# A first group of six products instead of four, fed by one load for each k-tile

## The chip, the cores and the metric

The kernel runs on one core of a Trainium2 chip. A core has TensorE (PE: matrix products and the loads of their weights), ScalarE (ACT), VectorE (DVE), GpSimd (POOL) and SyncE (SP, which issues most loads). The metric is the device time of one execution in microseconds (us), the median of several executions. The granted clock of TensorE averaged 0.995 of full speed, which is the 2.4 GHz level, in the profiled execution.

## What is computed

One inference step of a hybrid decoder layer for 256 prompt tokens and 8 sample tokens that share the weights. With NT = 264 columns of tokens and D = 2048:

```python
def _rmsnorm(x, g):
    x32 = x.astype(jnp.float32)
    y = x32 * lax.rsqrt(jnp.mean(x32 * x32, axis=-1, keepdims=True) + EPS) * g.astype(jnp.float32)
    return y.astype(x.dtype)
# h   = RMSNorm(x)
# z   = h @ w_in      (columns for the mLSTM heads, the sliding-window attention heads, two merge gates)
# A   = mLSTM matrix memory (4 heads, dk=256, dv=512)
# B   = sliding-window attention (32 query heads, 4 key/value heads, head_dim 64, window 128),
#       with sinks and partial rotary
# mix = (sigmoid(gA) * (A @ w_branch_a) + sigmoid(gB) * (B @ w_branch_b)) @ w_out
# x   = x + RMSNorm(mix)
# x   = x + RMSNorm(ConvFFN(RMSNorm(x)))
```

All is in 32-bit floating point. The kernel reaches that precision with three products for each weight tile: weights and activations are split into a rounded high part (`wh`, `xh`) and a remainder (`wl`, `xl`), and `wh·xh + wh·xl + wl·xh` is summed.

## The kernel before

Weights lie in memory as tiles of 128 x 128: an output tile of 128 columns has 16 of them, one for each k-tile of D. The function `product` (L86 to L117) makes n output tiles. It goes through chunks of at most eight weight tiles. For each chunk SP issues one load into `raw` (one of three buffers; L100), ACT casts `raw` to `wh` (L102), DVE forms `wl` as raw minus wh (L103), and PE does three matmuls of 128 x 128 by 128 x 264 for each tile into the accumulator `acc` (L111, L112, L113). `one` is `product` with a single output tile: two chunks of eight.

After a full chunk of eight `product` calls `step()`. It moves on the work that is dealt out between products: generators in `running`, each of which does a piece and yields, and generators in `waiting`, which are started one by one, seven steps apart (`launch` with a gap of 7). `drain` runs all that is left to its end, with no products between the pieces. The instructions of each engine are put into their final order by a scheduler that goes by priorities and by a model of durations.

The first group (L179) makes two key and two value tiles at once, in chunks of one k-tile, one, and then two. `load_x` issues the load of the pieces of x that the chunk needs, just ahead of the chunk's weights, on the same queue, and makes `xh` (ACT, L173) and `xl` (DVE, L174), with the weights of the norm in `gv`. The squares of x are summed into `xacc` (ACT L159, L162; DVE L163). Then `rstd_from` forms the reciprocal root mean square: 12 small matmuls `rs` (L147), a root on ACT, four steps on DVE (`rq`), matmuls and transposes that spread it over the columns (`rb`, L216, L218), and a copy to `rstd`. The tables of rotary cosines and sines in `katt` are multiplied by rstd (L232, L233). Keys go through `rope` (DVE and POOL), values through transposes `vt` (L266) into `VHL`.

Next come 16 products for the queries, four to a group g. Each goes through `rope` into `Qh` and `Ql`. After each group two generators `half` are launched, which do the attention of the prompt: scores `s` (L288, L290), softmax on ACT, transposes, products with the values, and at the end `hah` and `hal`, the split of the attention's output. Behind the eight of them `sample_attention` is launched, for the 8 sample tokens: scores `ss` (L369), softmax `es` and `Ps` (L379, L381), transposes `pst`, products `psp` and `psv` (L399, L404), sums and copies `hs` on DVE (L410, L412, L417) and the splits into `hah` and `hal`. Then follow the mLSTM gates, 16 products of the gate gB (their result is kept in `Bp`), and the products `qk_products(0)` for the first mLSTM head. Then `drain()` is called, four sigmoids of `Bp` are done on ACT (L748), and 16 products with the weights `wb` take `hah` and `hal` in place of `xh` and `xl`. ACT has the functions of its tables loaded in sets: a change from the exponential to the sigmoid shows as an `ACT_TABLE_LOAD`.

## Time and profile before

| | us |
|---|---|
| median of 3 executions | 1783.11 (1782.82 to 1787.02) |
| profiled execution, device time | 1782.28 |
| its span, first to last instruction | 1780.5 |
| PE busy in the span | 1749.1 |
| DVE busy | 1222.0 |
| ACT busy | 830.4 |
| first product matmul starts at | 5.07 |
| first matmul with hah starts at | 299.63 |

The span begins with the first instruction; what lies outside of it is 1.8 us. Busy time of an engine counts what it executes; a matmul's row lasts about 0.28 us, but matmuls overlap, so what a matmul costs is the distance from start to start. In the rows, a bracket at the end is the idle time of the engine before the instruction and what ended it; "<-" between two names reads "made from".

### The profile page before, as it was taken

What the parts mean: (1) busy time and instruction counts of PE and PEld (TensorE: products, weight loads), DVE (VectorE), ACT (ScalarE), POOL (GpSimd) and SP (SyncE); (2) the same over time, 40 slices, a digit from 0 to 9 for tenths busy, and PEclk for the clock granted to TensorE, in tenths of its full rate; (3) what the DMA queues carried; (4) which work ended last, traced back from release to release, by engine and by line L of the source; (5) the groups of instructions that cost most, each with busy time, mean ns of one, the idle gap of its engine ahead of it and who ended that gap; (6) DMA issues with size and microseconds to landing.
All of it is one profiled execution on the core that took longest, in us unless ns stands there. A gap on an engine that the chain in (4) does not pass through costs nothing.

```text
span 1780.5 us, 35035 instructions
## 1 busy us (share of the span) xinstructions
PE 1749.1 (98%) x14188; PEld 1733.7 (97%) x14188; DVE 1222.0 (69%) x2271; ACT 830.4 (47%) x1160; POOL 248.2 (14%) x438
## 2 busy tenths in 40 slices
PE   8999999999999999999999999999999999999996
PEld 8999999999999999999999899999999999999996
DVE  7788866556888798756643887777777777444443
ACT  6556555334555455444445544444444444434442
POOL 2542010000111121100021320000000001000001
PEclk9999999999999999999999999999999999999998
DMA  7444475655888888955555445555555555566563
GB/s 250 161 143 142 155 232 169 224 182 189 273 280 284 317 299 298 311 194 184 179 180 176 148 159 179 180 182 183 187 179 185 181 179 184 184 180 185 179 184 114
DMA packets 106587, 354.82 MB, mean 199 GB/s; under 512 B 11626, under 2 KB 20730, under 8 KB 106424
## 3 DMA queue, kind: packets, MB, share of 16 engines
q1 hardware_dynamic: 91672, 300.05, 51.0%
q0 software_dynamic: 14752, 52.52, 8.6%
q8 instruction: 111, 1.82, 0.4%
q14 instruction: 52, 0.43, 0.1%
HBM read 328.21 MB, written 24.32 MB: 198 GB/s over the span
## 4 chain that ended last, share of the span: by engine, by line
PE 84%; DVE 5%; DMA 5%; issue 2%; ACT 2%; POOL 2%; SPq 0%; POOLq 0%; ACTq 0%; DVEq 0%
PE acc L111 27%; PE acc L112 26%; PE acc L113 26%; DMA raw<-in_w_in 4%; DVE wl L103 2%; ACT wh L102 1%; POOL xs L847 1%; DMA katt<-in_katt 1%; DVE Ct L730 1%; PE s L288 0%; PE nc L668 0%; POOL qr L240 0%; PE pt L326 0%; DVE cj L733 0%; DMA out_c_s<-Ct 0%
## 5 line engine op out<-in xcount | busy, mean ns | idle before, releaser
L103 DVE TENSOR_TENSOR wl<-raw,wh 128x1024 fp32r<-128x1024 f32 (+1 forms) x569 | 694.5, 1221 | 418.3 <-ACT wh L102 414.9
L102 ACT CAST wh<-raw 128x1024 fp32r<-128x1024 f32 (+1 forms) x569 | 588.8, 1035 | 805.4 <-PE acc L112 587.4
L111 PE MATMUL acc<-xh,wh 128*128 128x264 f32 x1600 | 456.0, 285 | 2.8 <-ACT wh L102 2.8
L113 PE MATMUL acc<-xh,wl 128*128 128x264 f32 x1600 | 453.0, 284 | 1.9 <-DVE wl L103 1.8
L112 PE MATMUL acc<-xl,wh 128*128 128x264 f32 x1600 | 454.1, 284 | 0.1
L111 PE MATMUL acc<-h2h,wh 128*128 128x264 f32 x1408 | 399.9, 284 | 5.6 <-DVE E L862 3.4
L112 PE MATMUL acc<-h2l,wh 128*128 128x264 f32 x1408 | 401.2, 285 | 2.1 <-DVE h2l L852 1.9
L113 PE MATMUL acc<-h2h,wl 128*128 128x264 f32 x1408 | 399.7, 284 | 0.0
L111 PEld LDWEIGHTS acc<-xh,wh 128*128 128x128 f32 x1600 | 301.1, 188 | 4.6 <-ACT wh L102 3.4
L113 PEld LDWEIGHTS acc<-xh,wl 128*128 128x128 f32 x1600 | 300.5, 188 | 3.1 <-DVE wl L103 3.0
L112 PEld LDWEIGHTS acc<-xl,wh 128*128 128x128 f32 x1600 | 300.6, 188 | 0.7 <-DVE xl L174 0.3
L111 PEld LDWEIGHTS acc<-h2h,wh 128*128 128x128 f32 x1408 | 265.6, 189 | 6.0 <-ACT t L905 3.6
L112 PEld LDWEIGHTS acc<-h2l,wh 128*128 128x128 f32 x1408 | 265.3, 188 | 3.0 <-DVE h2l L852 3.0
L113 PEld LDWEIGHTS acc<-h2h,wl 128*128 128x128 f32 x1408 | 265.1, 188 | 0.0
L111 PE MATMUL acc<-yh,wh 128*128 128x264 f32 x704 | 200.0, 284 | 0.0
L112 PE MATMUL acc<-yl,wh 128*128 128x264 f32 x704 | 199.7, 284 | 0.0
L113 PE MATMUL acc<-yh,wl 128*128 128x264 f32 x704 | 199.5, 283 | 0.0
L111 PEld LDWEIGHTS acc<-yh,wh 128*128 128x128 f32 x704 | 132.5, 188 | 0.0
L112 PEld LDWEIGHTS acc<-yl,wh 128*128 128x128 f32 x704 | 132.5, 188 | 0.0
L113 PEld LDWEIGHTS acc<-yh,wl 128*128 128x128 f32 x704 | 132.3, 188 | 0.0
L833 POOL TENSOR_TENSOR nacc<-nacc,nsq 128x264 f32<-128x264 f32 x26 | 37.3, 1433 | 363.8 <-ACT nsq L826 349.0
L866 POOL COPY up_p<-E 128x2 f32<-128x2 f32 x88 | 19.6, 223 | 444.0 <-DVE E L862 444.0
(383 smaller groups left out, 2482.8 us busy)
## 6 DMA issues: line engine op xcount, KB each, us to landing
raw<-in_w_in SPq DMA_DIRECT2D x199, 512.0 KB, 4.7
raw<-in_wu SPq DMA_DIRECT2D x176, 512.0 KB, 3.6
raw<-in_wdn SPq DMA_DIRECT2D x80, 512.0 KB, 3.6
raw<-in_wb SPq DMA_DIRECT2D x32, 512.0 KB, 3.6
Ct<-in_c POOLq DMA_DIRECT2D x32, 512.0 KB, 8.5
out_c_s<-Ct POOLq DMA_DIRECT2D x32, 512.0 KB, 7.0
raw<-in_wa SPq DMA_DIRECT2D x32, 512.0 KB, 3.5
raw<-in_wo SPq DMA_DIRECT2D x32, 512.0 KB, 3.5
```

The source lines that it names most:

```text
L102: latest[0] = S.copy(out=wh[:, :m, :], in_=raw[:, :m, :])
L103: latest[1] = V.tensor_sub(out=wl[:, :m, :], in0=raw[:, :m, :], in1=wh[:, :m, :].bitcast(F32))
L111: T.matmul(ps[i][:, :NT], wh[:, w, :], h, start=kt == 0, stop=False)
L112: T.matmul(ps[i][:, :NT], wh[:, w, :], l, start=False, stop=False)
L113: latest[2] = T.matmul(ps[i][:, :NT], wl[:, w, :], h, start=False, stop=kt == K - 1)
L730: V.scalar_tensor_tensor(out=Ct[:, j, :], in0=kb[:, 256:512], scalar=wv[:, 4 * hd + j, bi:bi + 1], in1=Ct[:, j, :], op0=ALU.mult, op1=ALU.add)
L833: G.tensor_add(out=acc, in0=acc, in1=sq)
L847: x2add = (V if k1 <= 4 else G).tensor_add(out=x2, in0=x2, in1=m)
L866: G.tensor_copy(out=up_p[:, f, :], in_=e[:, 256:258])
```

## The change

There is a new input, `first`. For each k-tile it holds a row of 264 + 768 numbers in each of 128 partitions: x, and the six weight tiles of that k-tile for two key, two value and two query outputs (the last two of the 16 query tiles, 62 and 63). Sixteen buffers `piece` take it, one for each k-tile; the loads have a high priority. Piece 0 goes in two parts: its weights are issued by SP, its x and gv by ACT. The other 15 are issued by SP one after the other.

A new function `group` does the first group with six accumulators: four from the pool that products use and two from the other pool of PSUM banks. For each k-tile a function `first_chunk` makes xh and wh on ACT, xl and wl on DVE, and the squares of x on ACT; then come 18 matmuls. ACT's order within a k-tile is fixed: xh, wh, the square.

Behind the group its six results are copied: `kraw` for keys and values, `qraw` for the two queries. The first query product `q0` is called ahead of `rstd_from`, and the matmuls `rs` are held behind its first chunk. The V transposes move into a generator `values` that begins three steps later. For the last two queries of group g = 3, `qraw` is used and no product is made. So there are 14 query products instead of 16, and four calls of `step()` fewer ahead of `drain`.

```diff
+        def group(n, xh, xl, chunk):
+
+            ps = [pa.tile([128, 512], F32, tag="a", name="acc") if i < 4 else bank("acc") for i in range(n)]
+            for kt in range(KT):
+                wh, wl = chunk(kt)
+                h, l = xh[kt // 4][:, kt % 4, :], xl[kt // 4][:, kt % 4, :]
+                for i in range(n):
+                    T.matmul(ps[i][:, :NT], wh[:, i, :], h, start=kt == 0, stop=False)
+                    T.matmul(ps[i][:, :NT], wh[:, i, :], l, start=False, stop=False)
+                    latest[2] = T.matmul(ps[i][:, :NT], wl[:, i, :], h, start=False, stop=kt == KT - 1)
+                marks.append(latest[2])
...
+        pieces = [u(shape=(128, 1056), nm="piece") for _ in range(KT)]
+        with tc.high_priority(30000):
+            nc.sync.dma_start(out=pieces[0][:, NT:NT + 768], in_=a["first"][:, 0, NT:])
+            S.dma_start(out=pieces[0][:, 0:NT], in_=a["first"][:, 0, 0:NT])
+            S.dma_start(out=gv, in_=a["g"])
+            for k in range(1, KT):
+                nc.sync.dma_start(out=pieces[k][:, 0:NT + 768], in_=a["first"][:, k, :])
...
-        psk = product(WT[T_KA:T_KA + 4], 4, xh, xl, KT, [0, 1, 2, 4, 6, 8, 10, 12, 14, 16], load_x)
-        flush_squares()
...
+        def first_chunk(k):
...
+            scaled = S.activation(out=hi, in_=xk, func=AF.Copy, scale=gk)
+            V.scalar_tensor_tensor(out=lo, in0=xk, scalar=gk, in1=hi.bitcast(F32), op0=ALU.mult, op1=ALU.subtract)
...
+            latest[0] = S.copy(out=wh[:, 0:6, :], in_=raw)
+            paced(latest[0], scaled)
+            V.tensor_sub(out=wl[:, 0:6, :], in0=raw, in1=wh[:, 0:6, :].bitcast(F32))
...
+        psk = group(6, xh, xl, first_chunk)
...
-        rstd = rstd_from([xacc[:, 0, :], xacc[:, 1, :]], "rstd")
...
+        chunk = len(marks)
+        q0 = one(WT, T_QA, xh, xl)
+        rstd = rstd_from([xacc[:, 0, :], xacc[:, 1, :]], "rstd", after=[marks[chunk]] * 2)
...
+        def values():
+            for _ in range(3):
+                yield
...
+        running.append(values())
...
-                ps = one(WT, T_QA + 4 * g + i, xh, xl)
+                if g == 3 and i >= 2:
+                    ps = qraw[:, i - 2, :]
+                else:
+                    ps = q0 if g + i == 0 else one(WT, T_QA + 4 * g + i, xh, xl)
...
+    first = A["w_in"][[64, 65, 66, 67, 62, 63]].transpose(1, 2, 0, 3).reshape(128, 16, 768)
+    A["first"] = np.concatenate([A["x"], first], 2)
```

What it does to the order of instructions is shown at three places. The first is SP at the start of the program; before, the loads of x (`xr`) and of weights (`raw`) alternate:

```order
L167 DMA xr<-in_x 128x264
L169 DMA gv<-in_g 128x64
L100 DMA raw<-in_w_in 128x4x128
L167 DMA xr<-in_x 128x264
L100 DMA raw<-in_w_in 128x4x128
L167 DMA xr<-in_x 128x528
L100 DMA raw<-in_w_in 128x4x256
```

The same place of the changed kernel, with the loads of constants that follow the first group's:

```order
L148 DMA piece<-in_first 128x768
L152 DMA piece<-in_first 128x1032 x15
L100 DMA raw<-in_w_in 128x1024 x3
L207 DMA kc<-in_kc 128x256
L208 DMA katt<-in_katt 128x1714
L209 DMA bif<-in_bif 4x2
```

All pieces of the first group now stand ahead of everything else on SP; gv and the first piece of x are gone from its queue.

The second place is PE at the end of `qk_products(0)`, where the sample attention ends. Before, its first eight `psv` were followed by product matmuls, 24 of them up to the other eight; 72 more stand between those and the first product with hah:

```order
L112 MATMUL acc<-xl,wh 128x264
L113 MATMUL acc<-xh,wl 128x264
L399 MATMUL psp<-PsT,kc 128x256
L404 MATMUL psv<-PsT,vc 128x32 x8
L111 MATMUL acc<-xh,wh 128x264
L112 MATMUL acc<-xl,wh 128x264
L113 MATMUL acc<-xh,wl 128x264
```

In the changed kernel (`kq` and `ktk` are transposes of the first mLSTM head's keys and queries, which before stood between the products with hah):

```order
L112 MATMUL acc<-xl,wh 128x264
L113 MATMUL acc<-xh,wl 128x264
L429 MATMUL psp<-PsT,kc 128x256
L434 MATMUL psv<-PsT,vc 128x32 x16
L594 MATMUL kq_3949<-kc,qk 8x128 x4
L602 MATMUL ktk<-kc,qk 128x128 x4
L111 MATMUL acc<-hah,wh 128x264 x2
L112 MATMUL acc<-hal,wh 128x264
L113 MATMUL acc<-hah,wl 128x264
```

The product matmuls between and behind the `psv` have moved ahead of `psp`; between `psv` and the first product with hah stand eight transposes. In the same way 57 matmuls stand between `ss` and the first `pst`, where there were 72.

The third place is ACT over the same stretch. Before, the sample softmax (`es`, `Ps`) is done ahead of the sigmoids of Bp:

```order
L381 ACTIVATE Ps,sm<-ss,nb 128x129
L379 ACTIVATE es<-es 128x2
L381 ACTIVATE Ps,sm<-ss,nb 128x129
L102 CAST wh<-raw 128x1024 x4
L748 ACT_TABLE_LOAD
L748 ACTIVATE Bp<-Bp 128x1056
L123 CAST hah<-hs 128x4x8 x2
L102 CAST wh<-raw 128x1024
L123 CAST hah<-hs 128x4x8 x2
L748 ACTIVATE Bp<-Bp 128x1056 x2
```

After, the row that follows the last one here is that of the four casts to hah:

```order
L781 ACT_TABLE_LOAD
L781 ACTIVATE Bp<-Bp 128x1056
L409 ACT_TABLE_LOAD
L409 ACTIVATE es<-es 128x2
L102 CAST wh<-raw 128x1024
L411 ACTIVATE Ps,sm<-ss,nb 128x129 x2
L781 ACT_TABLE_LOAD
L781 ACTIVATE Bp<-Bp 128x1056
L102 CAST wh<-raw 128x1024
L781 ACTIVATE Bp<-Bp 128x1056
L102 CAST wh<-raw 128x1024
L781 ACTIVATE Bp<-Bp 128x1056
```

One sigmoid has moved ahead of the sample softmax, with two more table loads, and the other three stand ahead of the casts to hah. From the second matmul of the products with hah on, PE's order is the same as before to the end of the program.

## Rows read from the trace of the kernel before

**Rows 1.** The page's busy time by engine, and the chain that ended last.

```profile
PE 1749.1 (98%) x14188; PEld 1733.7 (97%) x14188; DVE 1222.0 (69%) x2271; ACT 830.4 (47%) x1160; POOL 248.2 (14%) x438
...
PE 84%; DVE 5%; DMA 5%; issue 2%; ACT 2%; POOL 2%; SPq 0%; POOLq 0%; ACTq 0%; DVEq 0%
```

**Rows 2.** Windows: us; busy (count) of PE, PEld, DVE, ACT, POOL; clock; DMA share; GB/s.

```profile
5.07:60.00 54.93, 51.59 (x409) 49.77 (x408) 42.84 (x80) 33.86 (x58) 14.77 (x19) 1.00 0.69 234
...
1200.00:1700.00 500.00, 500.00 (x4119) 500.00 (x4118) 322.72 (x499) 206.67 (x256) 41.73 (x121) 1.00 0.57 182
```

**Rows 3.** Waits of PE, 0 to 60 us: total, times, longest.

```profile
PE acc L111 <- ACT wh L102: 2.0, 2, 1.6
```

**Rows 4.** Timeline of the start: start, duration, engine, instruction, idle before and releaser.

```profile
3.11 0.52 ACT L173 ACTIVATE xh<-xr,gv 128x264 fp32r<-128x264 f32 x1 [0.87 <-DMA gv<-in_g]
...
4.30 0.62 ACT L102 CAST wh<-raw 128x512 fp32r<-128x512 f32 x1 [0.36 <-DMA raw<-in_w_in]
...
5.07 0.29 PE L111 MATMUL acc<-xh,wh 128*128 128x264 f32 x1
```

**Rows 5.** Groups by shape, 0 to 40 us: count, busy us, mean ns, idle before.

```profile
L103 DVE TENSOR_TENSOR wl<-raw,wh 128x1024 fp32r<-128x1024 f32 x11 | 13.3, 1220 | 3.4 <-ACT wh L102 3.4
L102 ACT CAST wh<-raw 128x1024 fp32r<-128x1024 f32 x11 | 11.5, 1047 | 6.2 <-DMA raw<-in_w_in 4.4 <-PE acc L112 1.6 <-DVE rq L212 0.2
L173 ACT ACTIVATE xh<-xr,gv 128x264 fp32r<-128x264 f32 x16 | 7.3, 507 | 1.6 <-DMA gv<-in_g 0.9 <-DMA xr<-in_x 0.7
L174 DVE SCALAR_TENSOR_TENSOR xl<-xr,gv,xh 128x264 fp32r<-128x264 f32 x16 | 7.2, 486 | 3.0 <-ACT xh L173 3.0
L163 DVE TENSOR_TENSOR xacc<-xacc,sq 128x528 f32<-128x528 f32 x7 | 4.9, 701 | 0.1
L162 ACT ACTIVATE sq<-xr 128x528 f32<-128x528 f32 x7 | 4.2, 630 | 0.0
...
L103 DVE TENSOR_TENSOR wl<-raw,wh 128x512 fp32r<-128x512 f32 x2 | 1.4, 693 | 1.2 <-ACT wh L102 1.2
...
L159 ACT ACTIVATE xacc<-xr 128x264 f32<-128x264 f32 x2 | 0.8, 408 | 0.0
```

**Rows 6.** Window of 10 to 15 us, columns as in rows 2.

```profile
10.00:15.00 5.00, 4.39 (x33) 4.18 (x34) 4.41 (x7) 5.00 (x9) 0.00 (x0) 1.00 0.87 286
```

**Rows 7.** DMA issues of the first 8 us: count, KB each, median us to landing.

```profile
raw<-in_w_in SPq DMA_DIRECT2D x3, 512.0 KB, 5.9
xr<-in_x SPq DMA_DIRECT2D x3, 264.0 KB, 6.1
```

**Rows 8.** Timeline: first use of rstd on DVE, first scores on PE.

```profile
37.41 0.42 DVE L232 TENSOR_TENSOR katt<-katt,rstd 128x264 f32<-128x264 f32 x1
...
62.57 0.40 PE L288 MATMUL s<-KZh,Qh 128*128 128x512 f32 x1
```

**Rows 9.** Timeline of PE around the end of the attention.

```profile
273.21 1.13 PE L369 MATMUL ss<-kT,qbd 128*32 128x129 f32 x32
...
280.21 0.38 PE L391 MATMUL pst<-kc,Ps 128*128 128x128 f32 x2
...
299.63 0.28 PE L111 MATMUL acc<-hah,wh 128*128 128x264 f32 x1
```

**Rows 10.** Timeline of ACT in the same stretch.

```profile
275.45 0.62 ACT L123 CAST hah<-pv 128x512 fp32r<-128x512 f32 x1
278.17 0.37 ACT L381 ACTIVATE Ps<-ss,nb 128x129 f32<-128x129 f32 x1 [2.10 <-DVE es L378]
...
290.21 1.28 ACT L748 ACT_TABLE_LOAD   x1
291.50 1.09 ACT L748 ACTIVATE Bp<-Bp 128x1056 f32<-128x1056 f32 x1
```

**Rows 11.** Timeline of DVE in the same stretch.

```profile
290.97 0.75 DVE L412 TENSOR_TENSOR hs<-hs,psv 128x256 f32<-128x256 f32 x2 [4.71 <-PE psv L404]
...
292.78 1.60 DVE L417 COPY hs<-hs 64x32 f32<-64x32 f32 x8
```

More of the change, by code (lines that the diff above doesn't have):

```diff
@@ L117, in product @@
             return [p[:, :NT] for p in ps]
+        def group(n, xh, xl, chunk):
[8 more added lines that the diff above has]
+                marks.append(latest[2])
+            return [p[:, :NT] for p in ps]
         def one(src, j, xh, xl, K=KT):
@@ L127, in build @@
         xh, xl = [u(F32R, nm="xh") for _ in range(4)], [u(F32R, nm="xl") for _ in range(4)]
-        xr = [u(nm="xr") for _ in range(4)]
         gv = kp.tile([128, 4, 16], F32, name="gv")
@@ L150, in squares @@
                     paced(mm, after)
-        pend = []
         xacc = u(shape=(128, 2, NT), nm="xacc")
-        def flush_squares():
-            for k0, k1 in pend:
-                xc = xr[k0 // 4][:, k0 % 4:k0 % 4 + k1 - k0, :]
-                if k1 <= 2:
-                    S.activation(out=xacc[:, k0:k1, :], in_=xc, func=AF.Square)
-                else:
-                    sq = u(shape=(128, 2, NT), nm="sq")
-                    S.activation(out=sq, in_=xc, func=AF.Square)
-                    V.tensor_add(out=xacc, in0=xacc, in1=sq)
-            pend.clear()
@@ L166, in load_x @@
-        def load_x(k0, k1):
-            nc.sync.dma_start(out=xr[k0 // 4][:, k0 % 4:k0 % 4 + k1 - k0, :], in_=a["x"][:, k0:k1, :])
-            if k0 == 0:
-                nc.sync.dma_start(out=gv, in_=a["g"])
-            for k in range(k0, k1):
-                xk, gk = xr[k // 4][:, k % 4, :], gv[:, 0, k:k + 1]
-                hi, lo = xh[k // 4][:, k % 4, :], xl[k // 4][:, k % 4, :]
-                S.activation(out=hi, in_=xk, func=AF.Copy, scale=gk)
-                V.scalar_tensor_tensor(out=lo, in0=xk, scalar=gk, in1=hi.bitcast(F32),
-                                       op0=ALU.mult, op1=ALU.subtract)
-            flush_squares()
-            pend.append((k0, k1))
@@ L179, in build @@
-        psk = product(WT[T_KA:T_KA + 4], 4, xh, xl, KT, [0, 1, 2, 4, 6, 8, 10, 12, 14, 16], load_x)
-        flush_squares()
+        sqs = []
+        def first_chunk(k):
+            xk, gk = pieces[k][:, 0:NT], gv[:, 0, k:k + 1]
+            raw = pieces[k][:, NT:NT + 768].rearrange("p (n c) -> p n c", c=128)
+            hi, lo = xh[k // 4][:, k % 4, :], xl[k // 4][:, k % 4, :]
+            wh = wp.tile([128, 8, 128], F32R, tag="wh", name="wh")
+            wl = wp.tile([128, 8, 128], F32R, tag="wl", name="wl")
+            scaled = S.activation(out=hi, in_=xk, func=AF.Copy, scale=gk)
+            V.scalar_tensor_tensor(out=lo, in0=xk, scalar=gk, in1=hi.bitcast(F32), op0=ALU.mult, op1=ALU.subtract)
+            if k:
+                paced(scaled, latest[0])
+            latest[0] = S.copy(out=wh[:, 0:6, :], in_=raw)
+            paced(latest[0], scaled)
+            V.tensor_sub(out=wl[:, 0:6, :], in0=raw, in1=wh[:, 0:6, :].bitcast(F32))
+            if k < 2:
+                paced(S.activation(out=xacc[:, k, :], in_=xk, func=AF.Square), latest[0])
+            else:
+                if k % 2 == 0:
+                    sqs.append(u(shape=(128, 2, NT), nm="sq"))
+                paced(S.activation(out=sqs[-1][:, k % 2, :], in_=xk, func=AF.Square), latest[0])
+                if k % 2:
+                    V.tensor_add(out=xacc, in0=xacc, in1=sqs[-1])
+            return wh, wl
@@ L226, in load_sqrt @@
             S.activation(out=tmp("w1", (128, 1)), in_=src, func=AF.Sqrt)
-        rstd = rstd_from([xacc[:, 0, :], xacc[:, 1, :]], "rstd")
+        kraw, kro, qraw = u(nm="kraw"), u(nm="kro"), u(shape=(128, 2, NT), nm="qraw")
+        for f in range(4):
+            S.copy(out=kraw[:, f, :], in_=psk[f])
+        for f in range(2):
+            S.copy(out=qraw[:, f, :], in_=psk[4 + f])
+        chunk = len(marks)
+        q0 = one(WT, T_QA, xh, xl)
+        rstd = rstd_from([xacc[:, 0, :], xacc[:, 1, :]], "rstd", after=[marks[chunk]] * 2)
         rot = list(range(8, 16)) + list(range(0, 8)) + list(range(16, 32))
@@ L244, in build @@
         VHL = u(F32R, (128, 2, 4, 128), "VHL")
-        kraw, kro = u(nm="kraw"), u(nm="kro")
         kvs = kp.tile([128, 4, NB], F32, name="kvs")
-        for f in range(4):
-            S.copy(out=kraw[:, f, :], in_=psk[f])
         for f in range(2):
@@ L425, in build @@
             for i in range(4):
[L426 removed]
+                if g == 3 and i >= 2:
+                    ps = qraw[:, i - 2, :]
+                else:
+                    ps = q0 if g + i == 0 else one(WT, T_QA + 4 * g + i, xh, xl)
                 qr = tmp("qr", tag="t3")
```

13 lines of the change are left out of this document (7 added, 6 removed).

## The prediction

> **What bounds the kernel now.** I read the page first. TensorE (PE) is busy 98% of the span, and the chain of work that ended last is PE for 84% [rows 1]. The windows give the engine's floor: from 1200 to 1700 us 4119 matmuls are recorded in 500.00 us of busy time, one in 0.1214 us [rows 2]. So a change pays only where PE starts its matmuls further apart than 0.1214 us. From the first product matmul to 60 us there are 409 in 54.93 us [rows 2]; at 0.1214 they need 49.65, so 5.28 us are lost there. That is all that the new first group can win. The waits of PE name the largest piece: 2.0 us in two waits for the cast `wh` [rows 3]; the rest are single short ones around the root mean square and the V transposes, and the first matmul after each.
>
> The cause is in the timeline [rows 4]: the weight cast at 4.30 waited for its load, and the engine that does it then has casts of x, squares and the next chunk in its queue. Loads are the deeper cause: in the stretch of 10 to 15 us the DMA engines are busy 0.87 of the time and move 286 GB/s [rows 6].
>
> **What the change does to the first 60 us.** The same matmuls run in another order: six accumulators, 18 matmuls per k-tile, so one k-tile buys PE 18 x 0.1214 = 2.19 us. What must be made ready in that time, from [rows 5]:
> - ACT: x cast 0.51, weight cast of 768 columns 0.83 (between 0.62 for 512 in [rows 4] and 1.05 for 1024), square 0.41: 1.75 us.
> - DVE: x remainder 0.49, weight remainder of 768 columns 0.96 (between 0.69 and 1.22), half of a 0.70 sum of squares: 1.80 us.
> - The load: 128 x 4128 bytes, 528 KB, at 286 GB/s [rows 6] 1.85 us.
>
> All three are below 2.19, so after the first k-tile PE should be the limit. In the kernel before, two k-tiles of four outputs bought 24 x 0.1214 = 2.91 us and asked ACT for 2 x 0.51 + 1.05 + 0.63 (the wide square, 1.5 times the narrow one) = 2.70, with less margin and with loads held back by free buffers.
>
> The start: ahead of the first matmul now lie 393 KB of weights, 135 of x and 33 of gv, 561 KB against 430 before, but in fewer loads. Before, gv had landed at 3.11, when the x cast began, and the weights at 4.30 [rows 4]. The weight cast is 0.21 longer (0.83 for 0.62); ACT now issues two loads itself ahead of its table load; I take it to be free at about 3.1, when before it waited for gv anyway. 131 KB more at 286 GB/s would be 0.46 later; half of that is already in flight, by the loads behind. I take the first matmul at 5.05 to 5.3, so from 0 to 0.2 lost. After four matmuls (0.49) PE stands at the first `wl`, which is ready 0.96 after the cast: 0.45 lost. The second piece lands about 1.5 to 1.85 after the first and needs 0.51 + 0.83 more: at most 0.2 lost. The rest of the places (12 matmuls of `rs`, four of `rb`, four transposes `vt`) cost something in switching: 0.2. Lost in all 0.9; **gain 5.28 - 0.9 = 4.4 us**. Bounds: nothing lost but the start gives 5.1; one late k-tile in each four (0.5 us each) gives about 2.5.
>
> Steps that come with it, at no cost: `rs` now stands behind 24 matmuls of the first query product instead of in the group, so the sum of squares is long done when PE gets there; `rb` follows 23 matmuls later (2.8 us), against 21 (2.55) before, so its wait goes. The V transposes run three chunks later and their users later still. The SP queue: 16 pieces stand ahead of three weight chunks, `kc` and `katt`. At 1.85 us each the pieces are in by 32 us, `katt` (with the chunks ahead 2.6 MB more) by about 41, and its first use comes behind rstd, at about 49. In the K chain everything behind rstd moves by about 12 us: the first DVE product with rstd at 37.41 to about 49.5, and the first scores from 62.57 [rows 8] to about 68, since product order gives them 24 us of matmuls in both. Of the 25.2 us between the two only 19 remain. The longest part of that chain is on POOL and I reckon its last piece done 1 us before the scores are due: covered, by little.
>
> **What it does to the end of the attention.** Two queries that no longer need their own product take away four chunks of eight k-tiles, and a chunk is also a step for the work that is dealt out between products. The sample attention was dealt its steps up to the end of the last key/query product; now four steps fewer exist, and what is left runs in `drain`, with no products between. The order shows the consequence: between the scores `ss` and the transposes `pst` PE has 57 matmuls instead of 72, and from `psp` to the first product with hah there is no product matmul at all, where before 24 stood between the halves of `psv` and 72 behind the second. Before, none waited: the first product with hah at 299.63 has no bracket [rows 9].
>
> First wait, at `pst`. On ACT the order now puts a sigmoid, and so a table load, ahead of the softmax's `es`, and another load to come back. From the end of `ss` (273.21 + 1.13 = 274.34) to the end of the hah cast (275.45 + 0.62 = 276.07) [rows 9, 10] 1.73 us; table load 1.28, sigmoid 1.09, table load 1.28, weight cast 1.05 [rows 5, 10]; then from the first Ps to `pst`, 280.21 - 278.17 = 2.04 [rows 9, 10]. Sum 8.47. PE has 57 x 0.1214 = 6.92: 1.55 us of wait, and a weight remainder that DVE takes in the middle can add 0.3; I take **1.7**. Behind `pst` on PE stand all the rest of the product, psv and every product with hah.
>
> Second wait, at the first product with hah. After the last `psv` DVE needs two additions (0.75) and eight copies (1.60) [rows 11], and the splits into hah and hal follow, for which I take 0.4: 2.75 us. PE has eight transposes, 1.0 by the cadence. The wait is 1.75, in one or two pieces: **1.8**. It could be more, since on ACT three sigmoids and two casts (5.4 us) and a third table load stand ahead of hah; by the sum above ACT is through 14 us after `ss` and psv ends at about that time.
>
> Seam in all **3.5 us**. Bounds: 1.8 (ACT's extra sigmoid is covered) to 5 (both chains late by another 0.75).
>
> **Sum.** Profiled execution 1782.28 (span 1780.5): - 4.4 + 3.5 = -0.9, 1781.4. The median of the runs shown is 1783.11, 0.83 above the profiled one, so the forecast is 1783.11 - 0.9 = **1782.2**. All later matmuls stand in the same order.
>
> **Rivals.**
> 1. *The seam is covered.* ACT's first sigmoid runs while PE is still in the 57 matmuls and the drained chain overlaps. For it: the seam is from chains worked out of single rows. Against: eight transposes cannot hide 2.75 us. Half of the seam gone and the full first gain, 1783.11 - 5.1 + 1.8 = 1779.8; wholly gone 1778.6. Chance 0.18.
> 2. *The first group is fed late, or the K chain is.* If ACT and DVE lose 0.1 us at each k-tile to waiting on one another, or the scores come 2 us later, the gain is 2 less: 1784 to 1785. For it: the 1 us of margin on POOL, ACT 1.75 and DVE 1.80 of 2.19. Chance 0.10.
> 3. *Loads in flight share the engines* (slower). With all loads issued at once up to eight are outstanding. If they moved side by side instead of one after the other, the first piece would be complete only when most of eight are: about 12 us instead of 4, 8 us later, time 1783.11 - 0.9 + 8 = 1790. It decides from about 1 us of delay (no gain left) and at 6.4 the time is 0.3% slower. Against it: in the first 8 us loads of 264 KB and of 512 KB issued alternately take the same time to land, 6.1 and 5.9 us [rows 7], which is what a queue gives, and the first ones were not held by later ones. Chance 0.06.
> 4. *Table switches cost more than their load.* In the row the table load takes 1.28 and the next activation starts 0.01 us after it [rows 10]; if a switch also had to empty the engine first, and that took as long again as the load (1.28), two additional switches on the way to `pst` would cost 2.6 more: 1784.8. Chance 0.04.
> The Trainium skill, "ScalarE: Activation LUTs", section "What ACT_TABLE_LOAD costs", states the latter: about 1283 ns for the load and about 1380 ns of drain, 2.66 us for a switch; by its figure two switches cost 2.8 more and the time would be 1785.0. The trace agrees on the load (1.28) and shows no drain in the row that follows.
>
> **How the numbers follow.** Forecast as above 0.62, rivals 0.18, 0.10, 0.06, 0.04. The range takes rivals 1, 2 and 4: 1778.3 to 1785.5. A difference of 0.3% is 5.35 us, about what a measurement of this kernel can tell from no change. Faster needs under 1777.8, more than all that is lost in the first 60 us: 0.06. Slower needs over 1788.5, rival 3 and a seam of twice the size: 0.08. Within: 0.86.
>
> **What would show it.** In the changed kernel's trace: first product matmul at 5.05 to 5.3, the group of 288 matmuls over at about 41 with one wait for `wl` near its start and no wait for a cast; `rs`, `rb`, `vt` unwaited; no wait at the first scores; at the end of the attention waits of PE for DVE's `Ps` at `pst` (1.7) and for hah or hal at the first branch product (1.8). No waits there would make rival 1 right, waits of PE through the first group rival 2 or 3, and an idle ACT after each table load rival 4.

## The result, and the profile after

The changed kernel takes 1799.37 us (median of 6 runs, 1796.28 to 1801.29), against 1785.07 of the kernel before in the same runs: a ratio of 1.0082, 95% interval 1.0068 to 1.0096. It is 14 us slower, where 1782.2 with a range up to 1785.5 was forecast. The profiled execution has a span of 1799.4 us, 18.9 more than that of before. (The medians are 14.3 apart: the profiled execution of the changed kernel is the slowest of its six, and that of before, 1782.28, lies 2.8 under the 1785.07.)

The windows say where. Us of the window, then busy us and (instructions) of PE, PEld, DVE, ACT, POOL, then granted clock, share and GB/s of the DMA engines; the first row answers to [rows 2], the next two are stretches inside it:

```profile
5.00:60.00 55.00, 43.00 (x314) 42.27 (x314) 31.55 (x52) 29.56 (x57) 4.05 (x4) 0.88 0.51 200
...
8.50:12.20 3.70, 3.66 (x18) 3.66 (x19) 3.12 (x5) 3.28 (x7) 0.00 (x0) 0.55 1.01 412
30.86:36.10 5.24, 5.24 (x24) 5.24 (x25) 5.13 (x9) 1.54 (x3) 4.05 (x4) 0.50 0.00 0
```

Where 409 matmuls were done up to 60 us before, it is now 314. The granted clock averages 0.88 in this stretch, and in two pieces of it is 0.50 to 0.55, the 1.2 GHz level. Of the waits of PE from 0 to 60 us (total, times, longest), these answer to [rows 3]:

```profile
PE acc L128 <- DVE wl L188: 10.0, 2, 9.8
PE acc L126 <- ACT wh L186: 2.0, 1, 2.0
```

One wait of 9.8 us for a weight remainder that DVE makes in 0.95. Why it was late stands in the timeline of DVE (start, duration, instruction, idle before and what ended it):

```profile
15.89 0.49 DVE L183 SCALAR_TENSOR_TENSOR xl<-piece,gv,xh 128x264 fp32r<-128x264 f32 x1
29.11 0.29 DVE L219 CAST kr__579<-kc 128x256 fp32r<-128x256 f32 x1 [12.73 <-DMA kc<-in_kc]
29.32 0.62 DVE L501 CAST sel<-kc 128x128 fp32r<-128x128 f32 x4
29.86 0.95 DVE L188 TENSOR_TENSOR wl<-piece,wh 128x768 fp32r<-128x768 f32 x1
```

The cast of a table of constants, `kc`, stands in DVE's queue in the sixth k-tile, behind its `xl` and ahead of its `wl`. Its load stands on SP behind all pieces and three weight chunks, and lands at 29.1. DVE works in order: the `wh` that the sixth `wl` needs had been ready since 17.2, as a row of ACT shows, but DVE waits 12.73 us at kc, and the `wl` with it.

```profile
16.33 0.83 ACT L186 CAST wh<-piece 128x768 fp32r<-128x768 f32 x1 [0.62 <-PE acc L127]
```

PE, which waits for that `wl`, goes on at half clock:

```profile
30.86 0.59 PE L128 MATMUL acc<-xh,wl 128*128 128x264 f32 x1 [9.80 <-DVE wl L188]
31.25 0.42 PE L126 MATMUL acc<-xh,wh 128*128 128x264 f32 x1
31.47 0.42 PE L127 MATMUL acc<-xl,wh 128*128 128x264 f32 x1
```

The starts are 0.22 us apart, where 0.1214 is the full rate. The start is late too. On ACT, which answers to [rows 4], the first x cast waits for gv, from the load that ACT issued itself:

```profile
6.25 0.52 ACT L182 ACTIVATE xh<-piece,gv 128x264 fp32r<-128x264 f32 x1 [3.10 <-DMA gv<-in_g]
...
7.54 0.39 PE L126 MATMUL acc<-xh,wh 128*128 128x264 f32 x1 [1.96 <-ACT wh L186]
```

The first product matmul starts at 7.54, not 5.07. So the 18.9 us of the two profiles add up as follows. Start 2.5. Half clock at 8.5 to 12.2: 18 matmuls in 3.70 us instead of 2.19, 1.5. The wait for kc 9.8, and the half clock behind it, 24 matmuls in 5.24 instead of 2.91, 2.3. A first wait for `wl` of 0.4 and, as the remainder, 1.4 us of switching and short waits up to the scores. These make 17.9, of which 5.3 were lost in the kernel before as well: 12.6 more. (The first scores start 24.2 us later than in [rows 8], at 86.80 instead of 62.57; 11.65 of it are the 96 matmuls of two queries that are now done earlier.) From the first scores to `ss` the same matmuls then take 213.90 us instead of 210.64, 3.3 more, of which 2.5 are waits at scores in the middle of the attention. From `ss` to the last product with hah it is 116.91, where 124.77 less the 96 matmuls is 113.12: the end of the attention costs 3.8. Sum 19.7; the rest of the program took 0.7 less than in the profile of before, which leaves the 18.9 but for rounding.

For these two stretches, the waits of PE from 130 to 320 us:

```profile
PE s L318 <- DVE PT L137: 1.7, 1, 1.7
PE s L320 <- DVE PT L137: 0.8, 2, 0.6
PE acc L112 <- DVE hal L137: 0.4, 1, 0.4
PE pst L421 <- DVE Ps L416: 0.2, 1, 0.2
```

The first two did not exist in the kernel before at this place. The last two answer to [rows 9]: both predicted waits at the end of the attention are there, but short. What makes the place dear is again the clock. It is at the lower level already in the short products ahead of the first product with hah (the first row), and behind it (the second):

```profile
316.10:317.20 1.10, 1.10 (x6) 0.76 (x4) 1.04 (x6) 0.22 (x1) 0.00 (x0) 0.50 0.69 205
...
317.60:322.70 5.10, 4.71 (x21) 4.40 (x21) 3.86 (x18) 1.13 (x5) 1.43 (x3) 0.50 0.10 36
```

21 matmuls in 5.10 us, of which 0.4 is the wait for hal; at the full rate they need 2.55.

### The profile page after: what moved, and what is told of

Same layout as the page of the kernel before. It is cut to its first block, busy times and chain, and to the rows that moved or that the text cites. A ratio compares the mean times of both kernels' runs of the same rounds, so it can differ in the third digit from the quotient of the medians.

```text
span 1799.4 us, 35044 instructions
## 1 busy us (share of the span) xinstructions
PE 1757.1 (98%) x14188; PEld 1741.7 (97%) x14188; DVE 1225.1 (68%) x2274; ACT 835.3 (46%) x1174; POOL 246.3 (14%) x438
## 4 chain that ended last, share of the span: by engine, by line
PE 84%; DMA 6%; DVE 6%; ACT 1%; issue 1%; POOL 1%; POOLq 0%; SPq 0%; ACTq 0%; DVEq 0%
PE acc L112 26%; PE acc L111 26%; PE acc L113 26%; DMA raw<-in_w_in 4%; DVE wl L103 2%; ACT wh L102 1%; DMA piece<-in_first 1%; DMA kc<-in_kc 1%; PE s L318 1%; PE acc L128 1%; PE acc L126 0%; PE acc L127 0%; PE nc L701 0%; DMA kqd<-k 0%; DVE Ct L763 0%
## 5 line engine op out<-in xcount | busy, mean ns | idle before, releaser
L103 DVE TENSOR_TENSOR wl<-raw,wh 128x1024 fp32r<-128x1024 f32 (+1 forms) x556 | 678.8, 1221 | 414.5 <-ACT wh L102 412.2
L102 ACT CAST wh<-raw 128x1024 fp32r<-128x1024 f32 (+1 forms) x556 | 576.2, 1037 | 800.7 <-PE acc L112 635.6
L113 PE MATMUL acc<-xh,wl 128*128 128x264 f32 x1504 | 427.5, 284 | 4.2 <-DVE wl L103 4.1
L111 PE MATMUL acc<-xh,wh 128*128 128x264 f32 x1504 | 429.2, 285 | 0.3 <-ACT wh L102 0.3
L112 PE MATMUL acc<-xl,wh 128*128 128x264 f32 x1504 | 427.3, 284 | 0.0
L113 PEld LDWEIGHTS acc<-xh,wl 128*128 128x128 f32 x1504 | 282.8, 188 | 5.7 <-DVE wl L103 5.7
L111 PEld LDWEIGHTS acc<-xh,wh 128*128 128x128 f32 x1504 | 283.0, 188 | 1.9 <-ACT wh L102 0.7
L112 PEld LDWEIGHTS acc<-xl,wh 128*128 128x128 f32 x1504 | 282.6, 188 | 0.4
```

Source lines behind the costliest of these rows:

```text
L102: latest[0] = S.copy(out=wh[:, :m, :], in_=raw[:, :m, :])
L103: latest[1] = V.tensor_sub(out=wl[:, :m, :], in0=raw[:, :m, :], in1=wh[:, :m, :].bitcast(F32))
L111: T.matmul(ps[i][:, :NT], wh[:, w, :], h, start=kt == 0, stop=False)
L112: T.matmul(ps[i][:, :NT], wh[:, w, :], l, start=False, stop=False)
L113: latest[2] = T.matmul(ps[i][:, :NT], wl[:, w, :], h, start=False, stop=kt == K - 1)
```

## The experiments

Theory: DVE stood at a constant whose load the change had put behind 8 MB of pieces; the other losses are gv, the clock behind each pause, and the four lost steps. Rivals: the group of six cannot be fed (by loads, ACT or DVE), or the loads in flight delay each other. All runs:

| kernel | us | before, same chip | ratio (95%) |
|---|---|---|---|
| the change | 1799.37 | 1785.07 | 1.0082 (1.0068 to 1.0096) |
| casts late | 1788.26 | 1783.65 | 1.0030 (1.0019 to 1.0042) |
| casts late, 34 matmuls on zeros (one execution) | 1785.55 | 1784.05 | none |
| x and gv first | 1801.15 | 1783.65 | 1.0115 (1.0086 to 1.0145) |
| both | 1783.82 | 1783.65 | 1.0008 (0.9993 to 1.0022) |
| both, gaps of six at the end | 1788.90 | 1783.65 | 1.0035 (1.0020 to 1.0049) |
| the same, ns late | 1783.39 | 1783.97 | 1.0002 (0.9988 to 1.0015) |
| gaps of six at the front, ns late | 1793.66 | 1783.97 | 1.0059 (1.0042 to 1.0075) |
| both, four products | 1781.84 | 1783.97 | 0.9987 (0.9976 to 0.9998) |
| constants' loads early | 1798.23 | 1783.97 | 1.0086 (1.0064 to 1.0107) |
| casts behind the tenth piece | 1791.71 | 1784.05 | 1.0035 (1.0021 to 1.0048) |
| four products, rstd as before | 1780.77 | 1784.05 | 0.9976 (0.9963 to 0.9988) |

The ratio is on record with its interval; it is not the quotient of the two medians. Behind the last product with hah all kernels do the same work, but in the profiles this part takes from 1376.7 us (gaps of six at the end) to 1385.1 (constants' loads early). So what an edit does is read in the profiles up to that product, and a difference of a few us between two total times needs its interval.

**Casts late.** The constants' casts are held behind the last `wl` of the group.

```diff
+        behind_group = latest[1]
-        V.tensor_copy(out=kr_[:, 512:768], in_=kc)
+        paced(V.tensor_copy(out=kr_[:, 512:768], in_=kc), behind_group)
```

The casts from katt and the copies `sel` are held in the same way.

> The changed kernel with one thing moved: the casts of the constants kc and katt and the copies sel are held on DVE behind the last wl of the first group. Theory (DVE stood at the cast of kc, whose load lies behind all pieces on SP): the wait of 9.8 us of PE goes, and with it the 25 matmuls at half clock behind it (25 x 0.1 = 2.4 us); 12 us less than the changed kernel, about 1787 us, DVE has no wait over 1.5 us in the group. Rival (the pieces themselves, or ACT and DVE, cannot feed the group, and the cast only happened to stand there): PE waits for other wl or wh instead, within 3 us of the changed kernel, about 1797 to 1800.

Measured 1788.26. In the profile the first scores come at 73.78 instead of 86.80, 13 us earlier, and of PE's waits up to 60 us that the view lists only one of 2.2 us, for the first cast of weights, remains beside the one at the very start. The first rows of the scores, of the change and of this kernel:

```profile
86.80 0.40 PE L318 MATMUL s<-KZh,Qh 128*128 128x512 f32 x1
```
```profile
73.78 0.40 PE L319 MATMUL s<-KZh,Qh 128*128 128x512 f32 x1
```

So the group of six can be fed, from the same loads in the same order: the casts were the cause.

**x and gv first.** The first piece of x and gv go out on SP ahead of the first weights.

```diff
-            nc.sync.dma_start(out=pieces[0][:, NT:NT + 768], in_=a["first"][:, 0, NT:])
-            S.dma_start(out=pieces[0][:, 0:NT], in_=a["first"][:, 0, 0:NT])
-            S.dma_start(out=gv, in_=a["g"])
+            nc.sync.dma_start(out=pieces[0][:, 0:NT], in_=a["first"][:, 0, 0:NT])
+            nc.sync.dma_start(out=gv, in_=a["g"])
+            nc.sync.dma_start(out=pieces[0][:, NT:NT + 768], in_=a["first"][:, 0, NT:])
```

> The changed kernel with the first piece of x and gv issued on SP ahead of the first weights, instead of on ACT's queue. Theory: gv was late (6.2 us) since its small rows share the engines with the pieces queued on SP; now it lands at about 3, the first product matmul starts at 5.3 to 5.8 instead of 7.5 and the half clock of the first 18 matmuls goes. But the wait for kc behind it swallows the gain, since kc lands at about 29 as before: within 1.5 us of the changed kernel, 1798 to 1800, and a wait of PE of 13 us instead of 9.8. Rival (the two losses add): 3.5 us less, about 1796.

Measured 1801.15, no faster than the change. The first product matmul starts at 6.33, later than the 5.3 to 5.8 expected (the 393 KB of weights now come last), 1.2 us earlier than in the change. But the wait for `wl` takes it up and more, with kc landing 1.6 us later than in the change (30.73 for 29.11):

```profile
PE acc L128 <- DVE wl L188: 14.3, 2, 14.0
```

A start that comes earlier in front of a fixed landing only makes the wait longer.

**Both.**

> Both edits together: constants' casts behind the group, x and gv first on SP. Theory: the losses of the start now count, 2.0 us of start and 1.4 us of half clock less than with the casts moved alone: about 1783.5, with the group at full cadence from 6 us on. Rival (clock and start were one cost with the wait): the same as with the casts moved alone, 1787.

Measured 1783.82. With the wait for kc gone, the same edit to the start is worth 4.4 us by the medians (1788.26 to 1783.82), where it was worth nothing before. Up to `ss` the profiles show 2.3 of it (286.43 for 288.75): 1.0 by the earlier first matmul (6.24 for 7.27) and 1.3 by the clock. From the first matmul to 30 us the clock is 1.00:

```profile
6.24:12.00 5.76, 5.52 (x43) 5.31 (x44) 5.33 (x8) 5.63 (x12) 0.00 (x0) 1.00 1.02 414
12.00:30.00 18.00, 18.00 (x150) 18.00 (x150) 14.41 (x23) 13.13 (x27) 3.75 (x4) 1.00 1.02 407
...
71.44 0.40 PE L319 MATMUL s<-KZh,Qh 128*128 128x512 f32 x1
```

This is the kernel that the prediction described, and its time is near the one named (1782.2): same as before within the interval. That is luck in part. In its profile the last product with hah starts at 403.98, 6.0 us behind before (397.98), where the sum had it 0.9 ahead: the first scores gain 2.8 (11.65 of the two queries taken off), from there to `ss` 4.35 are lost and at the end of the attention 4.4. The rest of the program then took 2.6 us less than in the profile of before, which no edit accounts for.

**The clock alone.** 34 instead of 18 matmuls on zeros ahead of the group, on top of the late casts, so that PE does not pause before the first product.

> The run with the casts of the constants moved alone, and 34 instead of 18 matmuls on zeros ahead of the first group, so that PE is busy until its first product matmul at about 7.3 us. One look. Theory (the half clock of the first products comes from PE's pause of 2 us before them, not from the products): no stretch at 0.22 us a matmul behind the start, and from the first product matmul to rs 38.3 to 38.6 us instead of 39.85. Rival (the clock is held down by what the products themselves draw at the start): the same 39.8.

From the first product matmul (7.42) to `rs` (46.00) 38.58 us; without them 39.85 (7.27 to 47.12). The windows from 7.3 to 12.2 us, first of this kernel, then of the one with late casts and 18:

```profile
7.30:12.20 4.90, 4.54 (x35) 4.33 (x36) 4.52 (x7) 4.90 (x12) 0.00 (x0) 1.00 1.02 415
```
```profile
7.30:12.20 4.90, 4.83 (x26) 4.52 (x27) 4.04 (x6) 4.34 (x10) 0.00 (x0) 0.65 1.02 416
```

The clock of 0.65 is gone when PE is busy until the products begin, with the same products behind: so it came from the pause, and cost 1.27 us beside the pause itself. This is a single execution, so its total of 1785.55 has no interval. How long a pause must be is not shown: in the run with gaps of six at the front the first products start 0.22 us apart behind a pause of 0.55.

**Dose.** The casts are held behind the `wl` of the tenth piece, not behind the group (in the change, the cast of kc stands ahead of the sixth `wl`).

```diff
+            remainders.append(V.tensor_sub(out=wl[:, 0:6, :], in0=raw, in1=wh[:, 0:6, :].bitcast(F32)))
...
+        behind_group = remainders[9]
```

> The changed kernel with the casts of katt and kc held on DVE behind the wl of the tenth piece instead of standing ahead of that of the seventh (not behind the whole group). Theory (PE's wait is the time from DVE's arrival to the landing of the load, no more): katt lands at about 31.2 as before, DVE comes to it at about 25, PE needs the eleventh wl at 29.8 and gets it at about 33: a wait of 3 us instead of 9.8, some 7 us less than the changed kernel, 1791 to 1793 against 1784 of the kernel before. Rival (the place of the cast does not matter as long as it is inside the group): 10 us of wait, 1798 to 1801; or none, 1788.

Measured 1791.71, in the expected 1791 to 1793. DVE arrives later at the cast and waits for katt, and PE for the next `wl`:

```profile
31.60 0.43 DVE L219 CAST kr__579<-katt 128x512 fp32r<-128x512 f32 x1 [4.20 <-DMA katt<-in_katt]
```
```profile
33.15 0.39 PE L128 MATMUL acc<-xh,wl 128*128 128x264 f32 x1 [1.69 <-DVE wl L188]
```

4.20 us instead of 12.73 on DVE, 1.69 instead of 9.80 on PE: the wait is the distance between arrival and landing, and the loads land within 0.4 us of when they did. The time came out as expected with a shorter wait than the 3 us named: DVE came to the cast at 27.4, not 25, and PE needed the eleventh `wl` at 31.5, not 29.8. The first scores stand at 75.73, 2.0 us later than with the casts behind the group; the medians are 3.5 apart.

**Constants' loads early.** On top of x and gv first, the loads of kc and katt are issued ahead of piece 8; the casts are left to the scheduler.

```diff
             for k in range(1, KT):
+                if k == 8:
+                    nc.sync.dma_start(out=kc, in_=a["kc"])
+                    nc.sync.dma_start(out=kt_, in_=a["katt"])
                 nc.sync.dma_start(out=pieces[k][:, 0:NT + 768], in_=a["first"][:, k, :])
```

> The changed kernel with x and gv first on SP, and the loads of kc and katt issued ahead of piece 8 instead of behind the group's and three more loads; the casts stay where the scheduler puts them on DVE. Theory (it is only the place of the loads against the place of the casts): no wait of PE for wl over 1 us in the group, as with the casts moved, about 1783 to 1785. Rival (casting constants in the group costs DVE what it has no time for, or 1 MB more ahead of piece 8 starves the group): waits for wl or wh of 3 us and more, 1787 or more.

Missed, and by the theory's own mechanism: 1798.23. The loads stand earlier in the program, and the scheduler, which expects them early, put the casts at the very front of DVE's queue, ahead of the first `xl`:

```profile
14.70 0.29 DVE L220 CAST kr__579<-kc 128x256 fp32r<-128x256 f32 x1 [13.49 <-DMA kc<-in_kc]
16.82 0.43 DVE L219 CAST kr__579<-katt 128x512 fp32r<-128x512 f32 x1 [1.28 <-DMA katt<-in_katt]
```

kc lands 14.4 us earlier than in the change, and DVE waits for it longer than there (13.49 for 12.73). The scheduler places a consumer by its own model and not by the landing; here, moving the load moved the consumer too.

**The lost steps.** The last four pieces of attention are launched six steps apart, so that the sample attention has its four steps back.

```diff
-            launch(half(g, 0, Qh, Ql), 7)
-            launch(half(g, 1, Qh, Ql), 7)
+            launch(half(g, 0, Qh, Ql), 7 if g < 2 else 6)
+            launch(half(g, 1, Qh, Ql), 7 if g < 2 else 6)
```

> As the one with both edits, and the last four pieces of attention are launched six steps apart instead of seven, so that the sample attention ends four steps earlier and product matmuls stand behind its last psv again (no products in between were lost; nothing is left out). Theory (the end of the attention costs 3.5 to 3.7 us by waits for hal and by the half clock behind it): 3.5 us less than with both edits, about 1780, slightly faster than the kernel before; no wait for hal, no stretch at half clock at the first products with hah. Rival (attention packed closer makes PE wait for its softmax elsewhere): no gain or up to 2 us slower, 1783 to 1786.

Missed: 1788.90, 5 us slower than without. The wait for hal went, but another came, at the transposes of the sample softmax; the rows of DVE and PE:

```profile
275.01 0.34 DVE L646 TENSOR_SCALAR ns<-ns,st 8x256 f32<-8x256 f32 x1 [4.74 <-DMA ns<-in_n]
```
```profile
284.93 0.44 PE L422 MATMUL pst<-kc,Ps 128*128 128x128 f32 x2 [3.72 <-DVE Ps L417]
```

It is the same thing again: `ns` is a state whose load stands on POOL's queue behind those of the sample attention, and DVE's scaling of it stands ahead of the sample softmax. But the profile does not show the 5 us: it is that of the fastest of ten executions (1782.57), and its last product with hah starts at 404.09, as with both edits alone (403.98). What the other executions lose stays open.

**The same, ns late.** The scaling of ns is held behind the sample softmax.

```diff
-            V.tensor_scalar(out=nh, in0=nh, scalar1=dc[:, hd:hd + 1], scalar2=None, op0=ALU.mult)
+            paced(V.tensor_scalar(out=nh, in0=nh, scalar1=dc[:, hd:hd + 1], scalar2=None, op0=ALU.mult), soft[0])
```

> The kernel with both edits and the four launch gaps of six, and one more edit: the scaling of ns, whose load on POOL's queue lies behind the caches of the sample attention, is held on DVE behind the sample softmax. In the run with the launch gaps DVE stood 4.7 us at ns, and PE 3.7 us at pst for it, with 17 matmuls at half clock behind (1.7 us). Theory (the same mechanism as at kc: a DVE operation on a late load stands ahead of one that PE needs): that wait and the half clock go, 5.5 us less than with the gaps alone, about 1783, and a further 0 to 3 us if the seam is then as in the kernel before: 1780 to 1783. Rival (the wait at pst is the packed attention's own): a wait of 3 to 4 us stays, 1787 to 1789.

Measured 1783.39: 5.5 us less, as expected, with a wait of 0.6 at `pst` in place of 3.72 and none for hal. In the profiles the edit is worth 3.1 us from `ss` to the last product with hah (126.94 for 130.05); where the rest of the 5.5 lies is not shown. And it is no better than both edits alone (1783.82, the intervals overlap). The theory wanted 3.5 us from the four steps. In the profiles, up to the last matmul with hah, it is 402.42 against 403.98, 1.6 us. A window shows where the rest stays, first of this kernel, then of the same products (behind the first eight `psv`) in the kernel before:

```profile
289.20:292.60 3.40, 3.40 (x17) 3.40 (x17) 0.17 (x1) 0.00 (x0) 0.00 (x0) 0.50 0.48 154
```
```profile
286.10:289.10 3.00, 3.00 (x28) 3.00 (x27) 0.17 (x1) 0.00 (x0) 0.00 (x0) 1.00 0.59 197
```

The clock is at its lower level behind the first `psv`, some 5 us after the wait at `pst`, and 17 matmuls take 3.40 us instead of 2.06: 1.3 us. Together with the wait that is 2 us of the 3.5.

**Gaps at the front.** The first four pieces are launched six steps apart, to move one of them off the gate product.

> As the run before it (constants' casts behind the group, x and gv first, ns behind the sample softmax), but the first four pieces of attention are launched six steps apart and the last four seven. Theory (the 2.5 us of waits at the scores at 148 to 152 us come from one piece of attention falling into the gate product, whose chunks have 32 matmuls instead of 48): moved off that product they go, 2 us less, about 1779 to 1781. Rival (DVE is the limit in the attention wherever it stands): the waits appear at another pair of scores, and the time is that of the run before it.

The rival was right, and more: 1793.66, 10 us slower. The waits at the scores did not go; they came at four pairs of scores:

```profile
PE s L321 <- DVE PT L137: 10.3, 4, 3.1
```

With these pieces of attention six steps apart, the scores of one meet DVE while it still splits the probabilities of the one before. For the first four pieces DVE needs the distance of seven steps; the last four, six steps apart in the two runs before, brought no new waits at scores.

**Four products.** Both edits; keys and values alone in the group, 16 query products, no step lost.

```diff
-        psk = group(6, xh, xl, first_chunk)
+        psk = group(4, xh, xl, first_chunk)
...
-                if g == 3 and i >= 2:
-                    ps = qraw[:, i - 2, :]
-                else:
-                    ps = q0 if g + i == 0 else one(WT, T_QA + 4 * g + i, xh, xl)
+                ps = q0 if g + i == 0 else one(WT, T_QA + 4 * g + i, xh, xl)
```

> Loads alone: both edits, but four products side by side instead of six (two keys, two values), no queries kept, 16 query products and so no step lost. Theory (keeping two queries costs the end of the attention 3.5 us and the scores in the gate product 2.5 us; the first group of four is limited by ACT at 0.51 + 0.62 + 0.41 = 1.54 us for 12 matmuls of 1.46, which costs 1 to 1.5 us over 16 k-tiles): 4.5 us less than with both edits and six, about 1779, faster than the kernel before by 4 us; no wait for hal and no half clock at the end of the attention. Rival (six products are what feeds the group): PE waits for wh or wl at every k-tile, 0.3 us each, and the time is 1784 or more.

Measured 1781.84, 0.13% faster than before (interval 0.9976 to 0.9998). The expected 1779 was 3 us too low, but the sign against six is right, though the two intervals touch. In the profile the first matmul with hah starts at 299.15 (before 299.63, both edits with six 304.11), so keeping two queries costs 5.0 us by that point, and 6.8 by the last one (397.19 against 403.98). That is less than the two losses in the profile of both edits (4.35 and 4.4), since the version with four loses some 2 us of its own: its first scores come 2.8 us ahead of before (59.76), its `ss` only 0.9 ahead (272.35).

**Four products, rstd as before.** `rs` is not held behind the first query chunk, and rstd is formed ahead of the first query product.

```diff
-        q0 = one(WT, T_QA, xh, xl)
-        rstd = rstd_from([xacc[:, 0, :], xacc[:, 1, :]], "rstd", after=[marks[chunk]] * 2)
+        rstd = rstd_from([xacc[:, 0, :], xacc[:, 1, :]], "rstd")
+        q0 = one(WT, T_QA, xh, xl)
```

> The version with four products and both edits, with rstd formed as in the kernel before (rs not held behind the first query chunk, and ahead of the first query product). Theory (the K chain starts 3 us earlier, so DVE's work for keys and values is through before the scores, and the waits for wl at 56 to 73 us shrink): 1 us less than the version with four, 1780 to 1781. Rival (the waits come from DVE's total of work in that stretch): the same, 1782, or slower by the wait at rs of 0.7 that the kernel before has.

Measured 1780.77, ratio 0.9976 (0.9963 to 0.9988): the fastest version, 3.3 us under the kernel before by the medians and 4.3 by the ratio. Against the version before it the intervals overlap; in the profiles its last product with hah comes 2.9 us earlier (394.34). The stretch of [rows 2], from its own first product matmul:

```profile
5.39:60.00 54.61, 54.45 (x437) 53.54 (x437) 46.41 (x90) 37.53 (x76) 20.08 (x26) 1.00 0.67 240
```

437 matmuls in 54.61 us, where 409 stood in 54.93; at 0.1214 they need 53.05, so 1.6 us are lost instead of 5.28. The waits of PE at 60 to 330 us for wl and scores are down to one of 1.1 and one of 0.8, those that the kernel before has too. How much of this gain is the loads, how much the fixed order on ACT and the constants' place behind the group, no run separates.

## Why the prediction was wrong

**The step that failed** is the sentence on the SP queue: that `katt` lands by about 41 and "its first use comes behind rstd, at about 49". The loads were placed rightly, and even landed earlier (kc 29.1, katt 31.2). But the first use of both is not the rotary table behind rstd, it is the casts to `kr_` and the copies to `sel`, which need no rstd, and those I did not look for. DVE's order of the changed kernel has them in the group:

```
L183 SCALAR_TENSOR_TENSOR xl<-piece,gv,xh 128x264
L219 CAST kr__579<-kc 128x256
L501 CAST sel<-kc 128x128 x4
L188 TENSOR_TENSOR wl<-piece,wh 128x768
```

The trace of before had the warning as well, a DVE row in which the same cast waits for the same load, behind the last work of the group:

```profile
32.37 0.29 DVE L200 CAST kr__444<-kc 128x256 fp32r<-128x256 f32 x1 [1.48 <-DMA kc<-in_kc]
```

I had shown the order of SP, PE and ACT, where the change was meant to act, and summed DVE's work for a k-tile without reading what else stood in its queue. The step cost 9.8 us, and the clock 2.3 more; taking it away alone brought the ratio from 1.0082 to 1.0030.

**The start** (0 to 0.2 us lost) was mis-sized: 2.5 us, and 1.3 to 1.5 for the clock. I let gv land as before (at about 3.1), because its 33 KB were few; on ACT's queue beside SP's big rows it landed at 6.2.

**Feeding the group** at one k-tile in 2.19 us was right. The profile of both edits shows no wait in the group behind its first `wl` (0.2 us) and the full clock. Its first scores stand at 71.44; less the 11.65 of the two queries that is 2.8 us ahead of before, of 4.4 predicted, and most of the rest is the start (6.24 instead of 5.05 to 5.3).

**The end of the attention**: 3.5 us predicted, 3.8 measured, but made up otherwise, so that the two agree is luck. The wait at `pst` was 0.2, not 1.7: the sum 8.47 began with 1.73 us from the end of `ss` to the end of the hah cast, taken from the kernel before, and here that cast ended 0.4 us after `ss`. (The 57 matmuls ahead of `pst` are right, but they are not fewer than before: by the trace 48 stood there, and 72 only up to `psp`.) The wait for hal was 0.4 and none shows for hah, where 1.8 was predicted. The rest is the half clock, which the sum did not have at all: 2.6 us over the first 21 products with hah (317.25 to 322.79), and 0.5 over the eight transposes ahead of them. In the profile with the casts late the clock did not fall there, and the place cost 1.8 us, with waits of 0.5 for hah and 0.7 for hal.

**Not in the sum**: the waits of 2.5 us at scores in the middle of the attention. The sum counts nothing where PE's order stays the same. Why DVE is late there stays open: the run that moved the pieces off the gate product made the waits longer.

**Two slips** changed nothing. A seam wholly covered, with the gain of 5.1, gives 1778.0 and not 1778.6. And the first scores, by the sum's own terms (62.57 + 11.65 - 4.4), come at 69.8 and not at about 68.

**Rivals.** The first did not come about, since the end of the attention cost 3.8 us. The second (fed late, or the K chain) was wrong in its mechanism: the first scores did not wait. The third was near, in that a load behind others was late, but the loads did land one after the other (the first pieces 1.3 us apart); what was late was the one at the end, and an engine that stood for it. Its price (8 us) and its sign were right for a reason that I had not seen. The fourth is refuted, in rows of ACT in the changed kernel:

```profile
302.27 1.28 ACT L781 ACT_TABLE_LOAD   x1
303.57 1.09 ACT L781 ACTIVATE Bp<-Bp 128x1056 f32<-128x1056 f32 x1
304.67 1.28 ACT L409 ACT_TABLE_LOAD   x1
305.96 0.20 ACT L409 ACTIVATE es<-es 128x2 f32<-128x2 f32 x1
```

A switch costs its 1.28 us; the next activation starts 0.01 to 0.02 us after it, and the load 0.01 after the activation ahead of it. The Trainium skill, "ScalarE: Activation LUTs", section "What ACT_TABLE_LOAD costs", adds 1.38 us of drain to a switch; the trace does not show it here.

**The chances.** With 0.08 for slower the one large risk of such a change had no place: that a load is moved behind many others, while what uses it stays where it is on an engine that everybody waits for.

## What to carry to other kernels

When loads are moved ahead on a queue, list every load that they pass, and for each of these find the first instruction that uses it, on every engine, and what stands behind that instruction there. An engine that works in order stops at the first operand that is late, however small the operation is, so constants belong behind the work that cannot wait; moving their loads was no cure here, where the scheduler then moved their use as well. And an early finish in front of a fixed landing is worth nothing: the edit to the start gave 0 us with the wait in place and 4.4 by the medians (2.3 in the profiles up to `ss`) without it.

## What was not expected of the hardware

A load of 33 KB in rows of 256 bytes on ACT's queue took 5.0 us to land, issued at 1.18; a piece of 516 KB in rows of 4128 bytes, issued on SP in the same moment, landed at about the same time (6.0). The same load took 1.8 us in the kernel before, on SP with one other ahead of it. The rows of DMA issues (KB, us to landing), of the change and of before:

```profile
gv<-in_g ACTq DMA_DIRECT2D x1, 32.0 KB, 5.0
```
```profile
gv<-in_g SPq DMA_DIRECT2D x1, 32.0 KB, 1.8
```

The Trainium skill, "DMA: Bandwidth & Descriptors", section "Queues, rings and completion order", says that an engine goes round between queues packet by packet; the late landing agrees with that, but no run here shows the packets, and none has small rows on ACT's queue without the pieces on SP.

The DMA engines moved 393 to 418 GB/s while the pieces ran, with rows of 4 KB and all loads issued ahead, against 286 that I had reckoned with from [rows 6]. Behind the first piece, no engine waited for a piece in the group of six with both edits.

The granted clock of TensorE fell to the 1.2 GHz level behind pauses that were not long: 2.0 us ahead of the first products, and 3.7 us at `pst` in the run with gaps of six at the end. At the end of the attention of the change it fell with no wait of more than 0.2 us since `ss`, while PE did short products (32 `psv` and eight transposes). The length of a single pause does not settle it. Behind a wait of 1.7 us at the same scores it fell in the profiles of casts late, both, and ns late, and stayed at the 2.4 GHz level in those of the change, x and gv first, and the casts behind the tenth piece; in the last it also stayed behind the 1.69 us for the eleventh `wl`. Two windows behind that wait, of both edits and of the change:

```profile
151.80:155.00 3.20, 3.20 (x14) 3.00 (x13) 2.18 (x5) 2.58 (x5) 1.88 (x5) 0.50 0.00 0
```
```profile
167.00:170.20 3.20, 3.20 (x25) 3.07 (x26) 1.99 (x4) 2.59 (x5) 2.08 (x5) 1.00 0.03 10
```

Such a fall cost 1.3 to 2.6 us each time.
